# Three pairs of k-tiles made with seven products, in place of two, in the v and z_a products of an encoder layer

## The chip, the cores and the metric

The kernel runs on one core of one Trainium2 chip. The metric is the device time in microseconds (us) of one execution. A core has five engines with a queue of instructions each, worked off in order: TensorE (PE, matrix products), VectorE (DVE), ScalarE (ACT), GpSimd (POOL) and SyncE (SP, which here only issues DMAs). They wait for each other through semaphores. SBUF holds the tiles in 128 partitions, PSUM has eight banks in which matrix products add up, and 16 DMA engines move data between DRAM and SBUF, or within DRAM.

## The reference

One layer of a bidirectional encoder: 256 tokens, 2048 channels. Cut to what matters here:

```
hn   = rmsnorm(x, norm_w)
proj = hn @ w_in                         # (256, 2048) x (2048, 18432)
q, v, f_fwd, f_bwd, z_a, b_gate, c_gate, h_b, z_b = split(proj)    # 2048 columns each
o_a  = hgrn2_bidirectional(silu(q), v, f_fwd, f_bwd, lb)           # 16 heads of 128, chunks of 64
o_a  = head_rmsnorm(o_a) * silu(z_a)
y_b  = b_gate * conv3(c_gate * h_b);  o_b = rmsnorm(y_b) * silu(z_b)
h    = x + concat(o_a, o_b) @ w_out
h    = h + (p @ w_ple) * sigmoid(h @ w_ple_gate)
out  = rmsnorm(h, final_norm_w)
```

All is float32.

## The kernel before, in words

**Products.** A float32 operand is split into a high part, rounded to PE's fast float32r format, and the rest. A product is then three matmuls: high by high, high by low, low by high. `Stream.split` (L101, L102) makes the parts of the weights: ACT casts `raw` into the high half of an `spl` tile, DVE subtracts it from `raw` for the low half. `Stream.get` works four parts of 1024 columns ahead of PE; there are five `spl` buffers and three `raw` buffers of 1 MB. `Stream.load` issues the weight loads on SP (L80, or L76 for sums), in the order of use; a load waits until its `raw` buffer has been split.

**Order of the work.** The activations are held split in `xs` (16 k-tiles of 128). For i = 0, 2, 4, 6, `two_pairs(i)` makes two pairs of heads, i and i + 1. First come the forward and backward forget gates and q of both (`gemm_in`, L401 and L403; six products with 16 k-tiles each), then v and z_a of both pairs of heads at once. For i = 0 this is `gemm_two`; for i = 2, 4, 6 it is `gemm_vz`, a "v/z_a stage" below: 256 tokens (two halves m) by 512 columns of v and 512 of z_a (n). Between the products stand the chunkwise recurrence (`mix_forgets`, `mix_pair`, `outputs`) and the gate. Then follow the convolution branch, the output projection, the gate and the last norm.

**Pairs of k-tiles.** `gemm_vz` goes through eight pairs of k-tiles, q = 0 to 7, in that order. A plain pair takes 2 x 2 x 2 = 8 products (24 matmuls). A pair named in `VZ_SUMS` is treated as a 2 x 2 by 2 x 2 block product and made with seven (21 matmuls) in `half` (L523 to L525 are the matmuls in `three`): three go into the four main PSUM banks `avz` directly, and four into extra banks (`ex`, `ey` and the two `scps`), where all such pairs of a stage add up. After the last such pair, the extra banks are combined into `vt` and `zt` (one ACT copy; DVE L446 to L449). After the last pair, the main banks are added to them (L453) and scaled on ACT (L456); the first two additions free the two banks that the next `gemm_in` begins with. In the first and last pair of a stage, all products of v come before those of z_a. The main banks of z_a were used by q before, so the first product of z_a waits for q's evacuation (L464). Between the two stand the scores (L711) and the cross products `cx` (L755), which are put in at tick 4.

**Sums.** The seven products need sums of the activations and sums of the weights. Those of the activations are made once, in `xsums` (`act_sums`, L508 and L511; `act_split`, L518 and L519), into the tile `xsum`, through a scratch tile `xd`. Those of the weights are made in DRAM, in a tile `vz`: `prepare` copies the pair's four blocks (four DMAs of 256 KB on SP, L306), and `add_up` makes the sums with accumulating DMAs on POOL in three steps (step 0: two DMAs, L314; steps 1 and 2: one each, L318). Each step waits on POOL's queue for the landing of the one before. `Stream.add_sums` then lists the loads of such a pair: three blocks of `w_in` (0.75 MB) and the four blocks of sums (1 MB), 3.5 parts of 1024 columns where a plain pair has two.

**Due times.** `tick()` counts k-tiles (or groups of three matmuls); `at(dt, fn)` runs fn that many ticks later, in the order of the program. The sums for stage i + 2 are scheduled by `two_pairs(i)`: `prepare` of the z-th pair at tick 50 + 10z, its steps at ticks 166, 196 and 220 (+ z) for i > 0, and at 98 + 6 step + z for i = 0; the 158 ticks of a `two_pairs` put the former into the next one. `xsums(z)` is scheduled by `two_pairs(2)` at 10 + 12z. The planner below the program still moves instructions ahead of their place where an engine is free by its own estimate; the DMAs of `prepare` and `add_up` keep the program's order.

On POOL stand, besides L314 and L318: the multiplication by the norms (`by_norms`, L468), `kc`, `qc` and `kx` of `mix_pair` (L692, L698) and the gate (L593, L614). ACT makes the sigmoids and logarithms behind L468 (L590, L599), and DVE L603 and q's evacuation (L464) behind those.

Of the kernel before, what the change touches and what calls it, by code (L numbers as in the profile page):

```python
# [115 lines left out]
def tile_hymba_encoder(  # L116
# [32 lines left out]
    ws = Stream(tc, rawp, splp, 3)  # L149


    VZ_ORDER, VZ_SUMS = range(8), (2, 5)
    dramp = ctx.enter_context(tc.tile_pool(name="dramp", bufs=1, space=bass.MemoryType.DRAM))
    vz_prepared = {}
    blocks = {}
# [1087 lines left out]
```

## Time and profile before

| what | value |
|---|---|
| median of 3 runs | 1115.87 us (1114.24 to 1116.77) |
| profiled execution, first to last instruction (its span) | 1115.1 us, 0.77 us under the median |
| mean granted TensorE clock of the profiled execution | 0.997 |
| v/z_a stages (i = 2, 4, 6) in the profiled execution, from | about 194, 313 and 432 us |
| DMA over the span | 277.76 MB, mean 249 GB/s |

No separate time of the profiled execution is given beside its span, so the span stands for it. A row of a group gives line, engine, operation, tiles (out<-in), shapes and count; then busy us and the mean ns of one; then the idle time before it and what ended it. A row of the timeline gives start, duration, and in brackets the engine's idle time before it and its releaser. A row of the chain of waits gives start, duration and what ran, each step released by the one above it. "L102" is a line of the kernel. A matmul's duration is its whole passage through PE; the next one starts before it ends.

### The profile page before, as it was taken

The page shows a single profiled execution, that of the slowest core. Times are in us where ns is not written, and L with a number is a line of the kernel's source. Part 1 is how long each engine was busy: PE and PEld are TensorE (multiplying, and loading weights), DVE is VectorE, ACT ScalarE, POOL GpSimd, SP SyncE. Part 2 cuts the span into 40 slices and gives each one's busy share as a digit, 9 for nine tenths or more (in the row PEclk, how much of TensorE's full clock was granted, in tenths as well). Part 3 has the DMA queues.
Part 4 walks back from the last instruction along what each step waited for, and adds up shares of the span by engine and source line. Part 5 has one row for each costly group of instructions (what it writes and reads, how often), then busy time and mean ns, then how long its engine had stood idle before and what let it go on. Part 6 is the DMA issues. An engine that isn't in the chain of part 4 may idle for free.

```text
span 1115.1 us, 16970 instructions
## 1 busy us (share of the span) xinstructions
PE 1105.0 (99%) x6464; PEld 951.2 (85%) x6464; DVE 826.7 (74%) x1088; ACT 671.6 (60%) x939; POOL 291.5 (26%) x239
## 2 busy tenths in 40 slices
PE   9999999999999999999999999999999999999997
PEld 8888888888888888888888888888888888888886
DVE  7899467786887778797658748855758878877673
ACT  6787567666875697565535534534446565565562
POOL 1045325105530525043333223423331000000101
PEclk9999999999999999999999999999999999999998
DMA  9775985668778966858999998999979987887532
GB/s 348 273 249 192 223 266 179 217 227 213 234 207 306 303 172 182 279 180 206 296 312 252 263 335 218 294 311 266 298 201 296 332 287 284 297 305 254 196 132 76
DMA packets 79121, 277.76 MB, mean 249 GB/s; under 512 B 7872, under 2 KB 22080, under 8 KB 60736
## 3 DMA queue, kind: packets, MB, share of 16 engines
q1 hardware_dynamic: 64800, 253.26, 65.3%
q0 software_dynamic: 13952, 23.07, 13.6%
q8 instruction: 51, 0.84, 0.3%
q10 hardware_dynamic: 288, 0.34, 0.1%
q14 instruction: 30, 0.25, 0.1%
HBM read 274.55 MB, written 48.23 MB: 289 GB/s over the span
## 4 chain that ended last, share of the span: by engine, by line
PE 94%; ACT 2%; DMA 2%; POOL 1%; DVE 1%; issue 0%; DVEq 0%; ACTq 0%; POOLq 0%
PE a L403 34%; PE a L401 18%; PE avz L523 3%; PE avz L524 3%; PE avz L525 3%; PE pg L1004 3%; PE pg L1003 3%; PE pg L1005 3%; PE pa L523 2%; PE pa L524 2%; PE pa L525 2%; DMA raw<-in_w_in_dram 2%; PE a L424 1%; PE a L422 1%; PE a L423 1%; PE pb_sc L524 1%
## 5 line engine op out<-in xcount | busy, mean ns | idle before, releaser
L102 DVE TENSOR_TENSOR spl<-raw,spl 128x1024 fp32r<-128x1024 f32 (+2 forms) x413 | 505.7, 1238 | 190.1 <-ACT spl L101 187.5
L403 PE MATMUL a<-xs,spl 128*128 128x512 f32 x1792 | 624.6, 395 | 0.0
L101 ACT CAST spl<-raw 128x1024 fp32r<-128x1024 f32 (+2 forms) x413 | 409.0, 1001 | 250.6 <-PE a L401 88.1
L401 PE MATMUL a<-xs,spl 128*128 128x256 f32 x1792 | 496.8, 280 | 0.0
L403 PEld LDWEIGHTS a<-xs,spl 128*128 128x128 f32 x1792 | 334.6, 187 | 75.4
L401 PEld LDWEIGHTS a<-xs,spl 128*128 128x128 f32 x1792 | 337.5, 189 | 1.8
L1120 POOL TENSOR_TENSOR hh<-hh,fw 128x512 f32<-128x512 f32 (+1 forms) x9 | 11.0, 1228 | 250.7 <-ACT gt L1119 248.0
L523 PE MATMUL avz<-spl,xs 128*128 128x512 f32 x156 | 61.0, 391 | 0.6 <-DVE qt L464 0.6
L525 PE MATMUL avz<-spl,xs 128*128 128x512 f32 x156 | 60.7, 389 | 0.0
L524 PE MATMUL avz<-spl,xs 128*128 128x512 f32 x156 | 60.7, 389 | 0.0
L463 ACT COPY r<-a 128x256 f32<-128x256 f32 x112 | 40.4, 367 | 33.4 <-PE a L401 33.3
L692 POOL TENSOR_TENSOR qc<-pf,ge 128x256 f32<-128x256 f32 x16 | 23.2, 1453 | 106.5 <-ACT ge L679 95.6
L1003 PE MATMUL pg<-spl,ht 128*128 128x512 f32 (+1 forms) x120 | 45.2, 377 | 0.0
L1004 PE MATMUL pg<-spl,ht 128*128 128x512 f32 (+1 forms) x120 | 45.1, 376 | 0.0
L1005 PE MATMUL pg<-spl,ht 128*128 128x512 f32 (+1 forms) x120 | 45.0, 375 | 0.0
L468 POOL TENSOR_TENSOR xf<-xf,rbc 128x1024 f32<-128x1024 f32 x8 | 22.0, 2750 | 73.4 <-DVE rbc L379 49.4
L101 ACT CAST spl<-early 128x1024 fp32r<-128x1024 f32 (+1 forms) x29 | 28.7, 990 | 19.6 <-PE pb_y L525 7.5
L102 DVE TENSOR_TENSOR spl<-early,spl 128x1024 fp32r<-128x1024 f32 (+1 forms) x29 | 32.9, 1147 | 9.4 <-ACT spl L101 8.7
L920 POOL TENSOR_TENSOR cg<-cg,hb 128x512 f32<-128x512 f32 x8 | 14.6, 1826 | 80.6 <-DVE hb L464 80.6
L523 PEld LDWEIGHTS avz<-spl,xs 128*128 128x128 f32 x156 | 29.3, 188 | 6.9 <-DVE qt L464 0.8
L523 PE MATMUL pa<-spl,mixa 128*128 128x512 f32 x88 | 34.5, 392 | 0.0
L525 PEld LDWEIGHTS avz<-spl,xs 128*128 128x128 f32 x156 | 29.3, 188 | 6.1
(322 smaller groups left out, 1637.8 us busy)
## 6 DMA issues: line engine op xcount, KB each, us to landing
raw<-in_w_in_dram SPq DMA_DIRECT2D x106, 1024.0 KB, 7.4
raw<-in_w_in_dram SPq DMA_DIRECT2D x88, 256.0 KB, 4.1
raw<-in_w_out_dram SPq DMA_DIRECT2D x36, 512.0 KB, 5.2
sums<-in_w_out_dram SPq DMA_DIRECT2D x32, 512.0 KB, 11.4
raw<-in_w_in_dram SPq DMA_DIRECT2D x26, 512.0 KB, 7.0
raw<-sums SPq DMA_DIRECT2D x13, 1024.0 KB, 6.0
raw<-in_w_gate_dram SPq DMA_DIRECT2D x9, 1024.0 KB, 5.5
sums<-in_w_out_dram POOLq DMA_DIRECT2D x16, 512.0 KB, 10.0
```

What stands on the lines that cost most here:

```text
L101: self.nc.scalar.copy(out=v[:, :, 0], in_=r)
L102: self.nc.vector.tensor_tensor(out=v[:, :, 1], in0=r, in1=v[:, :, 0], op=ALU.subtract)
L401: pe.matmul(a[:, :T], lhsT=lhsT, rhs=xs[:, kt, 0, :], start=False, stop=(kt == NKT - 1))
L403: pe.matmul(a, lhsT=lhsT, rhs=xs[:, kt, :, :].rearrange("p s n -> p (s n)"), start=(kt == 0), stop=False)
L463: act.copy(out=r, in_=acc[m][:, 1, :])
L523: pe.matmul(acc, lhsT=ah, rhs=w[:, 0], start=start, stop=False)
L524: pe.matmul(acc, lhsT=ah, rhs=w[:, 1], start=False, stop=False)
L525: pe.matmul(acc, lhsT=al, rhs=w[:, 0], start=False, stop=stop)
L692: pool.tensor_tensor(out=c64(dst[:, d]), in0=c64(src[:, d, :, half * P : (half + 1) * P]), in1=g.unsqueeze(3).broadcast_to([P, 2, 2, CH]), ...
L1003: pe.matmul(acc[m], lhsT=lh, rhs=wh, start=(kt == 0), stop=False)
L1004: pe.matmul(acc[m], lhsT=lh, rhs=wl, start=False, stop=False)
L1005: pe.matmul(acc[m], lhsT=ll, rhs=wh, start=False, stop=(kt == nk - 1))
```

## The change

The pairs 2, 4 and 6 are made with seven products in place of 2 and 5. All else follows from the length and the values of `VZ_SUMS`: a third sum of weights for each of the three stages, a third group of activation sums (`xsum` grows from 8 to 12 KB in a partition), a third set of due times.

```diff
-    VZ_ORDER, VZ_SUMS = range(8), (2, 5)
+    VZ_ORDER, VZ_SUMS = range(8), (2, 4, 6)
```

## The prediction

> **What bounds the kernel now.** I read the page first, then PE's waits, then windows by stage, then the chain of waits around the stages that change. The page and PE's waits:
>
> ```profile
> PE 1105.0 (99%) x6464; PEld 951.2 (85%) x6464; DVE 826.7 (74%) x1088; ACT 671.6 (60%) x939; POOL 291.5 (26%) x239
> q1 hardware_dynamic: 64800, 253.26, 65.3%
> q0 software_dynamic: 13952, 23.07, 13.6%
> PE wps L242 <- DVE wz L237: 1.1, 1, 1.1
> PE avz L523 <- DVE qt L464: 0.6, 1, 0.6
> ```
>
> TensorE is busy for 99% of the span. After the start it waits for another engine only once that the trace names: 0.6 us, at the second product of one v/z_a stage. So whatever PE no longer has to do is gained, and whatever makes PE wait is lost, one for one. The windows below are, in order, the three v/z_a stages (i = 2, 4, 6), with the two heads of q and f in front of the second (columns: us, then busy time and count of PE, PEld, DVE, ACT, POOL, then clock, share of the DMA engines, GB/s).
>
> ```profile
> 194.00:238.50 44.50, 44.50 (x276) 36.93 (x275) 33.12 (x36) 28.12 (x34) 4.54 (x4) 1.00 0.69 231
> 238.50:318.00 79.50, 79.44 (x615) 69.71 (x613) 61.89 (x90) 60.25 (x94) 35.99 (x26) 1.00 0.74 209
> 318.00:362.50 44.50, 43.92 (x199) 36.56 (x200) 34.73 (x39) 27.75 (x32) 4.54 (x4) 1.00 0.81 277
> 437.00:478.50 41.50, 41.50 (x188) 34.49 (x187) 31.72 (x34) 25.32 (x29) 6.01 (x7) 1.00 0.75 247
> ```
>
> The granted clock is 1.00, DVE is busy about three quarters of each v/z_a stage (33.12 of 44.50 us), and the DMA engines 0.69 to 0.81.
>
> **What the change removes.** Of a pair of k-tiles, eight products of three matmuls become seven: 24 matmuls become 21. The PE timeline of stage i = 4 has both kinds side by side: a pair with seven products runs from its first `ex` matmul at 326.88 to 331.63, the plain pair behind it to 337.07.
>
> ```profile
> 326.88 0.39 PE L523 MATMUL ex<-spl,xs 128*128 128x512 f32 x1
> 331.63 0.39 PE L523 MATMUL avz<-spl,xs 128*128 128x512 f32 x1
> 337.07 0.39 PE L523 MATMUL avz<-spl,xs 128*128 128x512 f32 x1
> ```
>
> The first is 4.75 us for 21, the second 5.44 us for 24, both 0.2265 us from start to start; the 0.39 us in the rows is one matmul's whole passage, and pricing by it would give 3.5 us, too much. One more such pair in each of three stages: 9 x 0.2265 = 2.04 us less PE work. That is all the change can give, apart from a wait that vanishes.
>
> **What it adds to DVE and ACT.** The third pair's activations are summed once (xsum), from rows of the two that exist:
>
> ```profile
> L511 DVE TENSOR_TENSOR xd<-xd x8: 280/288/1275, 45.8 to 60.8; 128x128 f32<-128x128 f32 x8
> L508 DVE TENSOR_TENSOR xd<-xs x2: 680/686/692, 45.1 to 46.9; 128x512 f32<-128x512 f32 x2
> L518 ACT CAST xsum<-xd x2: 614/614/615, 50.5 to 65.5; 128x512 fp32r<-128x512 f32 x2
> L519 DVE TENSOR_TENSOR xsum<-xd,xsum x2: 678/678/679, 58.4 to 74.8; 128x512 fp32r<-128x512 f32 x2
> 75.00:116.00 41.00, 41.00 (x346) 34.54 (x345) 37.69 (x47) 30.37 (x47) 23.86 (x20) 1.00 0.65 217
> ```
>
> DVE: 0.69 + 4 x 0.288 + 0.68 = 2.5 us, ACT 0.6 us. They share one scratch tile with the second pair's, whose last row starts at 74.8, so they fall in the stretch behind it, where DVE is busy 37.69 of 41 us. Its 3.3 us of idle time can hold them; if they land ahead of weight splits, PE could be late by at most 2.5 us. I take 0.2.
>
> A pair made with seven products splits 3.5 units of 1024 columns in place of 2:
>
> ```profile
> L102 DVE TENSOR_TENSOR spl<-raw,spl 128x1024 fp32r<-128x1024 f32 x369 | 477.0, 1303 | 186.3 <-ACT spl L101 183.7
> L102 DVE TENSOR_TENSOR spl<-raw,spl 128x512 fp32r<-128x512 f32 x40 | 28.1, 726 | 3.9 <-ACT spl L101 3.8
> ```
>
> On DVE 3 x 1.30 + 0.73 = 4.6 us against 2.6 us, under 4.75 us of PE time. In a stage DVE goes from about 33 to 35 of 44 us. No cost, with DVE's remaining 9 us as the cover.
>
> The pair's results are put together by one ACT copy and four DVE operations right after the last pair with seven products. That pair was 5, with two plain pairs (10.9 us) behind it; now it is 6, with one (5.44 us).
>
> ```profile
> 347.51 0.68 DVE L446 TENSOR_TENSOR xd<-vt,scps 128x512 f32<-128x512 f32 x1
> 350.44 0.68 DVE L449 TENSOR_TENSOR zt<-zt,scps 128x512 f32<-128x512 f32 x1
> 355.14 1.28 DVE L453 TENSOR_TENSOR vt<-avz,vt 128x512 f32<-128x512 f32 x2
> ```
>
> From the first to the end of the fourth is 3.6 us, one weight split among them. The two additions that free the first two PSUM banks (L453, 1.28 us) need these results. 3.6 + 1.3 = 4.9 us fits into 5.44 with half a microsecond over; one more split (1.2 us) in between costs 0.7 us in each stage. I take 0.2 in all; the end is 2.1.
>
> **What it adds to POOL and the DMA queues.** The third sum adds, for each stage, four copies from DRAM to DRAM on SP (1 MB), four accumulating DMAs of 256 KB on POOL in three steps (two, one, one), and 0.75 MB more to load. Where does that meet the path? The one PE wait is the place. The chain of waits that leads to it:
>
> ```profile
> 260.55 1.06 ACT spl L101
> 261.64 1.24 DVE spl L102
> 262.89 16.82 DMA raw<-in_w_in_dram
> 279.79 1.05 ACT spl L101
> ...
> 306.63 0.44 POOL kx L698
> 307.08 0.55 issue
> 307.63 1.67 POOL vz L318 x2
> 309.30 2.44 POOL xf L468
> ...
> 318.19 0.34 DVE qt L464
> 318.58 0.50 PE avz L523
> ```
>
> A weight load took 16.8 us, ACT got it late, and from there ACT, DVE and POOL pass the delay on for 38 us until q's evacuation frees PE's bank late. Two rows price that. ACT waited for the load at 279.79:
>
> ```profile
> 279.79 1.05 ACT L101 CAST spl<-raw 128x1024 fp32r<-128x1024 f32 x1 [0.82 <-DMA raw<-in_w_in_dram]
> 436.21 1.09 PE cx L755 x8
> 437.30 0.30 PE avz L523
> ```
>
> In stage i = 6, whose ACT has no such wait, PE goes from the cross products (436.21, eight) straight on at 437.30. So 0.82 us of ACT's wait became 0.64 us of PE's: the chain has 0.18 us of slack, and what comes on top is paid in full. Two things come on top.
>
> First, POOL issues three L318 where it issued two, between kx and the multiplication by the norms (xf L468). Two took 1.67 us on the chain, 0.83 each; in POOL's own rows the first starts at 307.63 and L468 at 308.72, 0.55 each. I take 0.55, in i = 4 in full, in i = 6 less the 0.18 of slack: 0.4. The stage i = 2 has its steps long before and pays nothing. Behind the waiting L318 of step 1, POOL's next work has cover:
>
> ```profile
> 274.71 0.85 POOL L318 DMA_DIRECT2D vz<-vz  x1 [4.22 <-DMA vz<-in_w_in_dram]
> 283.13 1.29 POOL L468 TENSOR_TENSOR qt<-qt,rbc 128x512 f32<-128x512 f32 x1 [7.58 <-DVE gx L677]
> ```
>
> A third wait there may last to 283 before anyone needs POOL.
>
> Second, the load itself. It was in flight while the step 0 DMAs of this stage and the copies for the next one were:
>
> ```profile
> 256.53 4.24 POOL L314 DMA_DIRECT2D vz<-in_w_in_dram  x4
> 262.00:270.00 8.00, 8.00 (x122) 7.04 (x121) 4.12 (x6) 4.45 (x6) 4.93 (x4) 1.00 1.13 246
> 270.00:278.00 8.00, 8.00 (x54) 7.22 (x52) 6.08 (x10) 7.06 (x13) 1.34 (x2) 1.00 0.96 250
> ```
>
> DMA share 1.13 and 0.96: full. Four L314 become six, 0.52 MB more. POOL's queue costs 13.6% of 1115.1 us for 23.07 MB, 6.6 us of all engines per MB: 3.45 us. The load is later by nothing if it gets through ahead of them, by 3.45 us if all of it goes first; both queues share the engines, so I take two thirds, nearer the upper end because the engines are full: 2.2 us. All of that reaches PE. The third copy for the next stage is issued 10 ticks behind the second, after the loads that matter here; in i = 6 no copies for a next stage stand beside step 0, and ACT had no wait for a load, so I charge nothing there.
>
> The Trainium skill's page "DMA: Bandwidth & Descriptors", section "Queues, rings and completion order", says that each DMA engine takes turns between the queues that have work, a packet at a time. By that rule POOL's packets do not simply go ahead of the load's, which supports a value between the two ends and against none. The same page's fit for a POOL DMA (section "Anatomy of one DMA"), 2.0 us plus bytes over 436 GB/s, would make 0.52 MB cost the engines about 1.2 us of movement (an estimate from that page) and two thirds of that, 0.8 us in place of 2.2, would bring the sum to 0.1 us above before, between my forecast and the second rival below; the trace's 6.6 us per MB speaks against that price for DMAs that accumulate.
>
> **The sum**, against the profiled execution's span of 1115.1 us: -2.04 (PE) + 0.55 + 0.4 (POOL) + 2.2 (load) + 0.2 (xsum) + 0.2 (end of stage) = +1.5 us, 1116.6. The median of the runs lies 0.8 us over the span, so 1117.4 us. A change under 0.2% (2.2 us) can hardly be told from none here, so this is no measurable change, on the slow side.
>
> **Rivals.**
> 1. *Slower: the late load is paid in full.* If step 0's extra 3.45 us all go ahead of the load, and ACT then also waits for the load behind it, the wait at i = 4's second product grows to about 4.6 us: -2.04 + 0.55 + 0.4 + 3.45 + 0.4 = +2.8 us, 1118.7 us; with one split in the way at each end of a stage another 2.1 us, 1120.8. It decides from a delay of 2.9 us on. For it: a share of 1.13, and a chain with no slack. Against: the load's queue was served all along. 0.40.
> 2. *The DMAs fit.* The load comes no later: -2.04 + 0.55 + 0.4 + 0 = -1.1 us, 1114.8 us. For it: POOL's two added DMAs queue behind four others. It shares the chance of "no change" with my forecast, 0.48 together, of which 0.14 is this one.
> 3. *Faster: the wait goes.* The stage in front is 0.68 us shorter, the engines' orders shift, and the load no longer falls into the full stretch: -2.04 - 0.64 = -2.7 us, 1113.2 us. Nothing in the rows moves these DMAs apart, 0.12.
>
> That the change doesn't do what it says would show as 24 matmuls for pair 4 or 6; the code leaves no room for it.
>
> **How the numbers follow.** Forecast 1117.4 us, no change 0.48, slower 0.40, faster 0.12. The likeliest case's own range is 1113.7 to 1118.1. The range, 1113.2 to 1122.0, reaches from the third rival to a little over the first with every end of a stage late.
>
> **What would show it.** Right: nine matmuls fewer; PE's wait at the second product of stage i = 4 between 2.5 and 4 us, with ACT's wait for a load near 280 grown from 0.82 to about 3; about 0.4 us of wait at i = 6; three L318 ahead of xf L468; no wait at the first f matmul after a v/z_a stage. Wrong: no growth of ACT's wait for the load, waits where a stage ends, or a wait near 100 us, where the splits are behind.

## The result, and the profile after

The change makes the kernel slower: 1123.26 us (median of 6 runs, 1120.16 to 1125.21) against 1115.99 us (6 runs of the kernel before, 1114.24 to 1116.77). The ratio is 1.0064, interval 1.0052 to 1.0075; the medians lie 7.3 us apart, and the new one lies outside the predicted range. The profiled execution of the changed kernel took 1121.36 us with a span of 1119.6 us, one of the quicker ones, so its span shows 4.5 us of the loss.

The page after (engines; then the two DMA queues: packets, MB, share of 16 engines) and PE's waits (us in total, times, longest):

```profile
PE 1102.5 (98%) x6455; PEld 948.5 (85%) x6455; DVE 832.8 (74%) x1100; ACT 676.5 (60%) x946; POOL 300.5 (27%) x251
q1 hardware_dynamic: 69264, 258.76, 65.7%
q0 software_dynamic: 16448, 26.22, 15.5%
```

```profile
PE avz L523 <- DVE qt L464: 2.9, 2, 1.9
PE avz L524 <- DVE spl L102: 1.8, 1, 1.8
...
PE cx L755 <- POOL kx L698: 1.1, 1, 1.1
PE a L401 <- DVE spl L102: 0.7, 1, 0.7
PE ogt L634 <- DVE ogz L624: 0.6, 1, 0.6
```

PE has nine matmuls fewer (6455 for 6464) and 2.5 us less busy time. But where it waited once after the start, for 0.6 us, it now waits six times, for 7.1 us in all (2.9 + 1.8 + 1.1 + 0.7 + 0.6). The work removed was as predicted; new waits are over three times as large. The PE timeline places the end points of the ledger below:

```profile
112.40 1.16 PE L755 MATMUL cx<-qc,kx 128*128 128x128 f32 x8 [1.06 <-POOL kx L698]
241.89 0.40 PE L403 MATMUL a<-xs,spl 128*128 128x512 f32 x1
323.78 0.50 PE L523 MATMUL avz<-spl,xs 128*128 128x512 f32 x1 [1.91 <-DVE qt L464]
342.28 0.39 PE L523 MATMUL ex<-spl,xs 128*128 128x512 f32 x1
352.48 0.39 PE L523 MATMUL ex<-spl,xs 128*128 128x512 f32 x1
442.84 0.50 PE L523 MATMUL avz<-spl,xs 128*128 128x512 f32 x1 [1.01 <-DVE qt L464]
```

```profile
241.60 0.40 PE L403 MATMUL a<-xs,spl 128*128 128x512 f32 x1
437.11 0.50 PE L523 MATMUL avz<-spl,xs 128*128 128x512 f32 x1
```

The first fence is after, the second before. From the first `ex` matmul of pair 4 to that of pair 6 lie 10.20 us: 45 matmuls (21 of a pair with seven products, 24 of the plain pair 5) at 0.2267 us, the predicted price. Early in the first product of the forget gates for i = 4, PE is 0.29 us later than before (241.89 against 241.60). At the second product of stage i = 4 it is 5.20 us later (323.78 against 318.58). So between these two points, which hold no matmul that the change touches, 4.9 us were lost. At the second product of i = 6 it is 5.73 us later, after 0.68 us gained in stage i = 4: 1.21 us more lost by then.

The chain of waits to the second product of stage i = 4 has the same steps as before, from another load:

```profile
272.28 20.42 DMA raw<-in_w_in_dram
292.78 1.05 ACT spl L101
...
311.05 1.05 POOL kx L698
312.10 2.43 POOL vz L318 x3
314.53 2.42 POOL xf L468
...
323.40 0.34 DVE qt L464
323.78 0.50 PE avz L523
```

A load issued at 272.28 takes 20.4 us, ACT gets it at 292.78, and the delay goes through ACT, DVE, POOL (three L318 between kx and xf) and q's evacuation to PE. ACT's own row, from its timeline, says how long it stood:

```profile
292.78 1.05 ACT L101 CAST spl<-raw 128x1024 fp32r<-128x1024 f32 x1 [4.93 <-DMA raw<-in_w_in_dram]
```

That is 4.93 us where before shows 0.82, at the load in front of this one: 4.1 us more. With one more L318 in the chain (2.43 us for three against 1.67 for two, 0.8 us) this makes 4.9 us, what PE lost between the two points.

What delays the load is read from the two queues while it was in flight, 272.4 to 286.3 before and 272.3 to 292.7 after (packets, MB, share of the 16 engines; before is the upper fence):

```profile
q1 hardware_dynamic: 1575, 3.93, 84.4%
q0 software_dynamic: 298, 0.53, 21.6%
```

```profile
q1 hardware_dynamic: 1911, 4.33, 62.5%
q0 software_dynamic: 1229, 1.54, 45.9%
```

In both the two queues fill the engines. What went through SP's queue (q1) in that time is nearly the same: 84.4% of 13.9 us is 11.7 us of all engines before, 62.5% of 20.4 us is 12.8 after. But after, POOL's queue (q0) has twice the share, and SP's takes longer for much the same work. The Trainium skill's page "DMA: Bandwidth & Descriptors", section "Queues, rings and completion order", has the engines take turns between the queues, a packet at a time. The trace agrees in so far as both queues move at once; it shows no fixed shares (62.5 to 45.9 here, 34.7 to 76.7 in e7 below).

### The profile page after: what moved, and what is told of

Its sections match the earlier page's. It is cut to its first block, busy times and chain, and to the rows that moved or that the text cites. A ratio compares the mean times of both kernels' runs of the same rounds, so it can differ in the third digit from the quotient of the medians.

```text
span 1119.6 us, 17020 instructions
## 1 busy us (share of the span) xinstructions
PE 1102.5 (98%) x6455; PEld 948.5 (85%) x6455; DVE 832.8 (74%) x1100; ACT 676.5 (60%) x946; POOL 300.5 (27%) x251
## 3 DMA queue, kind: packets, MB, share of 16 engines
q1 hardware_dynamic: 69264, 258.76, 65.7%
q0 software_dynamic: 16448, 26.22, 15.5%
## 4 chain that ended last, share of the span: by engine, by line
PE 78%; DVE 8%; POOL 5%; ACT 3%; DMA 2%; issue 2%; SPq 0%; DVEq 0%; ACTq 0%; POOLq 0%
PE a L403 28%; PE a L401 15%; DVE spl L102 3%; PE pg L1004 3%; PE pg L1005 3%; PE pg L1003 3%; PE avz L523 2%; PE avz L525 2%; PE avz L524 2%; DMA raw<-in_w_in_dram 2%; PE pa L523 2%; PE pa L524 2%; PE pa L525 2%; POOL kc L692 1%; POOL xf L468 1%
## 5 line engine op out<-in xcount | busy, mean ns | idle before, releaser
L101 ACT CAST spl<-raw 128x1024 fp32r<-128x1024 f32 (+2 forms) x419 | 414.0, 999 | 251.2 <-PE a L401 92.5
L401 PE MATMUL a<-xs,spl 128*128 128x256 f32 x1792 | 496.5, 280 | 0.7 <-DVE spl L102 0.7
L401 PEld LDWEIGHTS a<-xs,spl 128*128 128x128 f32 x1792 | 337.6, 189 | 3.2 <-DVE spl L102 1.3
L523 PE MATMUL avz<-spl,xs 128*128 128x512 f32 x138 | 54.1, 392 | 2.9 <-DVE qt L464 2.9
L524 PE MATMUL avz<-spl,xs 128*128 128x512 f32 x138 | 53.8, 390 | 1.8 <-DVE spl L102 1.8
L525 PE MATMUL avz<-spl,xs 128*128 128x512 f32 x138 | 53.8, 390 | 0.0
L468 POOL TENSOR_TENSOR xf<-xf,rbc 128x1024 f32<-128x1024 f32 x8 | 22.6, 2828 | 70.9 <-DVE rbc L379 48.8
L523 PE MATMUL pa<-spl,mixa 128*128 128x512 f32 x88 | 34.5, 392 | 0.0
L524 PE MATMUL pa<-spl,mixa 128*128 128x512 f32 x88 | 34.3, 390 | 0.0
L525 PE MATMUL pa<-spl,mixa 128*128 128x512 f32 x88 | 34.3, 390 | 0.0
```

The costliest lines, as they stand in the source:

```text
L101: self.nc.scalar.copy(out=v[:, :, 0], in_=r)
L401: pe.matmul(a[:, :T], lhsT=lhsT, rhs=xs[:, kt, 0, :], start=False, stop=(kt == NKT - 1))
L468: pool.tensor_tensor(out=t, in0=t, in1=r.unsqueeze(1).broadcast_to([P, n, T]), op=ALU.mult)
L523: pe.matmul(acc, lhsT=ah, rhs=w[:, 0], start=start, stop=False)
L524: pe.matmul(acc, lhsT=ah, rhs=w[:, 1], start=False, stop=False)
L525: pe.matmul(acc, lhsT=al, rhs=w[:, 0], start=False, stop=stop)
```

## The experiments

Ratios are against the kernel before on the same chip, with 95% intervals; line numbers in some kernels stand one to four higher than in the listing. The theory at this point: the DMAs of the third weight sum delay the load, and ACT, DVE and POOL hand the delay to PE. The rivals: more work on DVE and ACT (splits, `xsum`); and the ends of the stages, where one plain pair is left in place of two.

### Without the third weight sum: e1_sums_shared

```diff
-                    sums = dramp.tile([P, 4, 512], F32, name=f"vz{i}_{q}")
-                    vz_prepared[i].append((srcs, sums))
+                    if q == 6:
+                        sums = vz_prepared[i][1][1]
+                    else:
+                        sums = dramp.tile([P, 4, 512], F32, name=f"vz{i}_{q}")
+                        vz_prepared[i].append((srcs, sums))
```

> Pairs 2, 4 and 6 with seven products, but the third pair's weight sums are not made: pair 6 loads the sums of pair 4 (that part of the output is wrong). All matmuls, splits, activation sums and loads are those of the changed kernel; the third sum's four copies and four accumulating DMAs per stage are gone. Theory (the third sum's DMAs delay a weight load of the heads before stage i = 4, and POOL's third L318 adds 0.5 us): most of the loss goes; left are -2.0 us of PE work, +1.4 us near 106 us and about +0.5 us at the ends of stages: within 1 us of the kernel before, 1115 to 1117 us; ACT's wait for a load near 280 us back under 1 us. Rival (the extra DVE and ACT work of the third pair makes the loss): 1121 to 1124 us as the changed kernel.

1116.06 us, ratio 0.9986 (0.9971 to 1.0002). By the ratios this is 8.7 us less than the change. ACT waits for no load between 265 and 305, the load of that place took 12.8 us, and of PE's waits after the start and up to the stages' end these are left:

```profile
PE cx L758 <- POOL kx L701: 1.1, 1, 1.1
PE avz L526 <- DVE qt L467: 0.2, 1, 0.2
```

All splits, loads and matmuls of the third pair are there; only the making of the sums is not. So these DMAs make the loss at i = 4. The 1.1 us at `cx` stay as they were in the change and must have another cause.

### The third sum made and not used: e2_dmas_alone

In the kernel before, pair 6 stays plain, but its weight sum is made:

```diff
+                if q == 6:
+                    vz_prepared[i].append((srcs, dramp.tile([P, 4, 512], F32, name=f"vz{i}_{q}")))
```

> The kernel before (pairs 2 and 5), and beside it a third sum of weights (of pair 6) is made in DRAM for each stage at the changed kernel's due times, but nothing reads it. Theory: the loss of the DMAs alone shows without any gain: +5 to +7 us against the kernel before, 1121 to 1123 us, with PE's wait at the second product of stage i = 4 at 4 us or more in place of 0.6. Rival (the work on DVE and ACT makes the loss): +0 to +1.5 us, 1116 to 1117.5 us.

1123.33 us, ratio 1.0043 (1.0027 to 1.0059). Nothing is added to PE, and nothing to DVE and ACT, and the waits around stage i = 4 are the change's (ACT's timeline, then PE's waits):

```profile
292.10 1.05 ACT L101 CAST spl<-raw 128x1024 fp32r<-128x1024 f32 x1 [5.00 <-DMA raw<-in_w_in_dram]
```

```profile
PE avz L525 <- DVE qt L466: 2.6, 2, 1.9
PE avz L526 <- DVE spl L102: 1.8, 1, 1.8
```

The rival of DVE's and ACT's work falls for the wait at i = 4. The DMAs alone cost 4.8 us (3.0 to 6.6), a little less than the 5 to 7 expected.

### Without the third group of activation sums: e3_no_third_xsum

The changed kernel, with pair 6 reading pair 4's activation sums (the two lines that point it there and shrink `xsum` are left out here):

```diff
-            for z in range(len(VZ_SUMS)):
+            for z in range(2):
```

> The changed kernel without the third group of activation sums: pair 6 uses those of pair 4 (that part of the output is wrong). 2.5 us of DVE work and 0.6 us of ACT work between 75 and 110 us are gone. Theory (these sums cost 1.4 us near 106 us, since the splits there have no slack left): 1.4 us faster than the changed kernel, 1120 to 1122.5 us, with PE's waits before 125 us as in the kernel before. Rival (they are hidden, and the shift near 106 us has another cause): 1123 us as the changed kernel.

1122.62 us, ratio 1.0043 (1.0026 to 1.0060). Its interval overlaps that of the change (1.0052 to 1.0075), so the time alone doesn't settle the third `xsum`. The trace does: the wait of `cx` for kx is gone from PE's waits, while those of i = 4 stay (`avz` 1.7 for a split). So the third group of sums makes the wait at 112 us.

### The last pair moved, without a third: e4_pairs_2_6

```diff
-    VZ_ORDER, VZ_SUMS = range(8), (2, 5)
+    VZ_ORDER, VZ_SUMS = range(8), (2, 6)
```

> Two pairs with seven products as before, but 2 and 6 in place of 2 and 5. Only the place of the second pair moves: its combination on DVE has one plain pair behind it, not two. Theory (the ends of the stages cost 0.2 to 0.5 us in all): +0 to +1 us against the kernel before, 1115.5 to 1117 us. Rival (the late combination holds up each stage's end by a split or more): +2 us or more, 1118 us, with PE's waits at the first f product behind each stage.

1115.77 us, ratio 0.9988 (0.9974 to 1.0002). One plain pair is left behind the last sum, as in the change, and PE waits at no end of a stage. Even before's 0.6 us is missing here: that small wait comes and goes between programs with equal DMAs. The ends of the stages as such are no cause.

### Which of the DMAs: e5_copies_alone and e6_copies_step0

Both are e2 with the third sum begun and not finished: `prepare` alone, or `prepare` and step 0 (two of its four accumulating DMAs). The lines below are e5's; e6 has `step >= 1`.

```diff
+                    if z == 2 and step >= 0:
+                        continue
```

> The kernel before, and of a third sum only its four copies from DRAM to DRAM per stage (1 MB, on SP), at the changed kernel's due times; no accumulating DMAs, nothing reads it. Theory (POOL's step 0 DMAs ahead of the load issued near 272 us are what delays it; the third copies are issued behind the loads that matter): within 1 us of the kernel before. Rival (the copies load the engines as much as the accumulation and make half of the loss): +2 us or more.

> As e5, and step 0 of the third sum as well (two accumulating DMAs of 256 KB per stage on POOL); no steps 1 and 2. Theory: step 0 carries most of the loss: +3 to +5 us against the kernel before, with ACT's wait for a load near 285 us at 3 us or more; missing against all the DMAs alone are POOL's third L318 ahead of the multiplication by the norms (0.55 us in i = 4, 0.4 in i = 6) and step 1's share of the engines. Rival (the loss sits in steps 1 and 2, that is in POOL's waiting): within 1 us of the kernel before.

e5: 1115.59 us, ratio 0.9998 (0.9988 to 1.0008). e6: 1120.94 us, ratio 1.0035 (1.0016 to 1.0054). The same load in e5, then in e6, with ACT's wait for it in e6:

```profile
raw<-in_w_in_dram SPq DMA_DIRECT2D x1, 1024.0 KB, 15.0
```

```profile
raw<-in_w_in_dram SPq DMA_DIRECT2D x1, 1024.0 KB, 19.2
```

```profile
291.23 1.05 ACT L101 CAST spl<-raw 128x1024 fp32r<-128x1024 f32 x1 [4.17 <-DMA raw<-in_w_in_dram]
```

The copies, 1 MB for each stage, cost nothing: they are issued behind the loads that matter. Step 0, 0.5 MB on POOL's queue, brings the delay (14.0 us before, 15.0 with copies, 19.2 with step 0) and most of the loss. PE's wait at i = 6 is absent in e6, so it belongs to steps 1 and 2.

### The copies moved out of the way: e7_copies_later and e8_before_copies_later

The load stands on SP's queue behind eight copies of the first two sums for stage i + 2, issued between 258 and 268, just when step 0 for stage i runs. e7 is the changed kernel, e8 the kernel before, with all copies 30 ticks later:

```diff
-                at(50 + 10 * z, lambda what=what: prepare(what))
+                at((80 if i else 50) + 10 * z, lambda what=what: prepare(what))
```

> The changed kernel with the copies for the next stage due at ticks 80, 90 and 100 in place of 50, 60 and 70 (for i > 0). All the work is kept; copies and step 0 no longer stand beside each other in front of stage i = 4. Theory (copies and step 0 together fill the engines and delay the loads by 20 us): the wait for the load goes, what is left of the loss is POOL's third L318 (1 us) and 1.4 us near 106 us, against 2.0 us gained: 1115 to 1118 us. Rival (POOL's accumulation alone delays the loads): 1121 us or more.

> The kernel before (pairs 2 and 5) with the same later due times of the copies. Theory: PE's 0.6 us of wait at stage i = 4 goes and nothing else changes: -0.3 to -1 us against the kernel before. Rival (the copies then delay the loads of the v/z_a stages instead): slower by 1 us or more, with PE waits inside a v/z_a stage.

e7: 1117.95 us, ratio 1.0017 (1.0007 to 1.0027). e8: 1116.51 us, ratio 1.0003 (0.9994 to 1.0012). The load in e7, and what is left of PE's waits at the second products:

```profile
raw<-in_w_in_dram SPq DMA_DIRECT2D x1, 1024.0 KB, 7.9
```

```profile
PE avz L523 <- DVE qt L464: 1.7, 2, 1.0
```

All six accumulating DMAs of step 0 still run, and the load takes 7.9 us in place of 20.4. In e8, with four of them, it takes 6.8. So neither step 0 nor the copies do it alone. While e7's load was in flight (274.8 to 282.7), SP's queue had even less of the engines than in the changed kernel:

```profile
q0 software_dynamic: 702, 0.99, 76.7%
q1 hardware_dynamic: 146, 1.06, 34.7%
```

But 34.7% of 7.9 us is 2.7 us of all engines, for little more than the load itself (1.06 MB), where 11.7 and 12.8 us went through SP's queue with the copies in front. Without them 5.2 us of the loss are gone (1.0064 less 1.0017). The kernel before, with four accumulating DMAs in step 0 and not six, gains nothing that can be measured, though PE's 0.6 us of wait is gone from e8's trace: the -0.3 to -1 us expected don't show. The waits at 112 us and at i = 6 stay.

### The rest of the loss: e9_and_xsum_later, e10_and_step2_early, e11_two_pairs_both_moves, e12_changed_again

e9 is e7 with the third group of activation sums kept in its place in the program, tick 34 of i = 2. e10 is e9 with step 2 of stages 4 and 6 issued ahead of POOL's kc in place of behind kx. e11 has pairs 2 and 5 with the copies later and step 2 early. e12 is the change again. The lines below are those of e9 and, behind the dots, of e10; the line that skips step 2 in its old place is left out.

```diff
-                act_sums(xs[:, k : k + 2], a, t)
+                act_sums(xs[:, k : k + 2], a, t, tc.keep_in_program_order if z == 2 else lambda instr: instr)
...
                     if before:
                         before()
+                    for what in vz_prepared[i] if i > 2 else ():
+                        add_up(what, 2)
```

> The changed kernel with the copies due later (as e7), and the third group of activation sums kept at its place in the program (tick 34 of i = 2, about 145 us, where DVE is half idle). Theory (they cost 1.4 us near 106 us): 1.4 us faster than with the copies alone moved: 0 to -1 us against the kernel before, with no shift of PE near 106 us. Rival (the shift there comes from elsewhere, or the sums cost as much at 145 us): as e7, +1.9 us.

> As e9, and step 2 of the sums for i = 4 and 6 is issued on POOL ahead of kc, in 3.6 us in which POOL waits for DVE, in place of between kx and the multiplication by the norms. Theory (each L318 there costs PE 0.55 to 0.83 us at the second product of stages i = 4 and 6): -2 to -3 us against the kernel before, 0.998, with no PE wait for DVE's qt; this would be the version that beats both kernels. Rival (those waits are made by DVE's or ACT's work): as e9.

> The kernel before (pairs 2 and 5) with the two moves that apply to it: copies later and step 2 ahead of kc. Theory (two L318 and the late load were all that PE waited for): -0.5 to -1 us against the kernel before, 0.9993; the third pair (e10) is then worth 2 us with everything else alike. Rival (the moves speed up two pairs as much as three): -2 us.

> The changed kernel itself, on the same chip as the three above. Theory: 1.0064 as measured, between 1.004 and 1.008, and between 1118 and 1126 us from one execution to the next, since the late load's delay differs. Rival (its loss is a matter of the chip): outside that.

| kernel | median us | ratio | interval |
|---|---|---|---|
| e9, + third xsum later | 1117.86 | 1.0004 | 0.9990 to 1.0018 |
| e10, + step 2 early | 1116.54 | 0.9994 | 0.9982 to 1.0005 |
| e11, two pairs, both moves | 1116.33 | 0.9991 | 0.9979 to 1.0003 |
| e12, the change | 1124.19 | 1.0061 | 1.0041 to 1.0081 |

e12 repeats the loss. Its profiled execution has a span 2.9 us longer than that of after, and shows a part that after's lacks: behind PE's wait at the second product of i = 4 the granted clock is 0.50 for some 3.4 us, and eight matmuls start 0.43 us apart in place of 0.23, 1.6 us more (columns as in the prediction's windows; e12, then after):

```profile
327.00:330.00 3.00, 3.00 (x9) 2.32 (x8) 3.00 (x5) 2.55 (x5) 1.73 (x3) 0.50 0.71 247
327.00:330.00 3.00, 3.00 (x15) 2.49 (x14) 3.00 (x4) 2.06 (x4) 2.96 (x3) 1.00 0.25 93
```

Four of the fourteen profiled executions have such a stretch around this stage's second product (e3, e6, e10, e12), and how often it comes in the other runs isn't recorded. So what PE loses at this place is at times more than its wait; what decides it isn't shown.

In e9 the wait of `cx` is gone, as in e3. In e10 the one of i = 6 is gone as well, but the one at i = 4 grows from 0.7 us in e9 to 1.7 (PE's waits, then the loads issued from 299 to 303):

```profile
PE avz L523 <- DVE qt L464: 1.7, 1, 1.7
```

```profile
raw<-in_w_in_dram SPq DMA_DIRECT2D x4, 256.0 KB, 12.1
```

Step 2 (issued from 294 on) now meets the later copies (issued from 295 to 297), and the next group of loads pays (ACT waits 2.93 us for one of them): 12.1 us for 256 KB, where the changed kernel's loads of that size, issued at 305 to 307, take 3.9. The moves together bring the third pair back to the time of before and no further; the -2 to -3 us expected of e10 fail. With the same moves, three pairs (e10) and two (e11) take the same time within their intervals: in the profiled execution of e10, 1.7 us go into this one wait and 1.6 into the matmuls at half the clock behind it, more than the third pair's 2.0 us. No kernel here is faster than before by more than its interval.

## Why the prediction was wrong, step by step

The kind of mechanism was predicted, a late load handed on through ACT, DVE and POOL, and so were the nine matmuls. What failed above all is the term of the load: it was worked out for another load, and by a rule for the delay that doesn't hold. Every other term of cost was too small as well.

- **PE, -2.04: right.** 45 matmuls in 10.20 us, and nine fewer of them.
- **The load, 2.2: the step that failed.** The prediction followed the load issued at 262.89, whose lateness the chain of before showed, and gave it two thirds of 3.45 us. In after that load takes 16.0 us (before 16.8) and ACT no longer waits for it. It is the next one, issued at 272, that goes from 14.0 to 20.4 us, and ACT's wait for a load from 0.82 to 4.93 us: 4.1 us in place of 2.2, and above the bound of 3.45. The bound was wrong too: it took step 0's engine time alone as the delay. The load grew by 6.4 us, because steps 0 and 1 of three sums follow each other on POOL's queue and leave SP's 62.5% of the engines in place of 84.4%, while the load stands behind eight copies on its own (e5, e6, e7). The prediction had this load as "the load behind it" in its first rival, without a price of its own. The fit of the Trainium skill's page "DMA: Bandwidth & Descriptors", section "Anatomy of one DMA", which would have made the term 0.8 us (an estimate from that page), is further off still. Step 1's waits on POOL's queue (timeline of after) show how long that queue stayed busy:

```profile
259.11 6.32 POOL L314 DMA_DIRECT2D vz<-in_w_in_dram  x6
280.10 0.84 POOL L318 DMA_DIRECT2D vz<-vz  x1 [6.57 <-DMA vz<-in_w_in_dram]
284.76 0.81 POOL L318 DMA_DIRECT2D vz<-vz  x1 [3.82 <-DMA vz<-in_w_in_dram]
```

  The third wait ends at 284.76, with 283 named as the latest time at which nobody needs POOL; the multiplication behind it (L468) started at 285.31, still ahead of the load that ACT waited for.
- **L318, 0.55 and 0.4: too small.** On the chain three take 2.43 us in i = 4 and two took 1.67: 0.76, not 0.55. The chain's own row (0.83 each) was the nearer one, as it counts what POOL's successor waits for. At i = 6 PE lost 1.21 us and not 0.4; one more L318 explains some 0.8 (three take 2.45 us on the chain there). The experiments tell the remaining 0.4 apart: by PE's timelines e2, with the third sum and none of the third pair's work, loses 0.9 us there, and e1, with the work and not the sum, 0.4. So it comes with the pair's own work; which instruction makes it was not followed.
- **xsum, 0.2: wrong.** PE loses 1.4 us at the third group of activation sums. The prediction had named "a wait near 100 us, where the splits are behind" as a sign against it. The cover it took, 3.3 us of idle time of DVE between 75 and 116, is an average over two stretches. Cut at 100.2, where DVE reaches the product that kc waits for, the same trace of before says (columns as above, DVE third):

```profile
72.00:100.20 28.20, 28.20 (x207) 23.52 (x206) 28.00 (x43) 22.95 (x31) 10.55 (x9) 1.00 0.63 208
100.20:116.00 15.80, 15.80 (x157) 13.63 (x156) 12.69 (x13) 10.20 (x20) 13.30 (x11) 1.00 0.76 263
```

  28.00 of 28.20 us are busy ahead of that point; all the idle time lies behind it. After, DVE's rows for the third group stand in the full part, and POOL's kc starts later by them (timeline after; the last row is before's kc):

```profile
75.57 0.49 DVE L511 TENSOR_TENSOR xd<-xd 128x128 f32<-128x128 f32 x2
77.11 0.61 DVE L511 TENSOR_TENSOR xd<-xd 128x128 f32<-128x128 f32 x2
91.74 0.68 DVE L519 TENSOR_TENSOR xsum<-xd,xsum 128x512 fp32r<-128x512 f32 x1
102.33 3.35 POOL L692 TENSOR_TENSOR kc<-dd,ge 128x256 f32<-128x256 f32 x1 [6.21 <-DVE pf L684]
```

```profile
100.89 3.35 POOL L692 TENSOR_TENSOR kc<-dd,ge 128x256 f32<-128x256 f32 x1 [6.22 <-DVE pf L684]
```

  The three rows make 1.78 us; kc is 1.44 us later, though PE ran 0.55 us earlier than before at that place. PE loses 1.44 us by the product behind the cross products, 1.06 us of it as the wait for kx. The place was right ("the stretch behind it"), its price was not: what matters there is DVE's own path, not whether weight splits come late.
- **Ends of the stages, 0.2: a little small.** At i = 6 one split (478.23) does get between the four operations, as the prediction had it, and the first additions (L453) start at 481.15, late by a part of a microsecond:

```profile
478.23 1.22 DVE L102 TENSOR_TENSOR spl<-raw,spl 128x1024 fp32r<-128x1024 f32 x1
```

```profile
481.51 0.39 PE L525 MATMUL avz<-spl,xs 128*128 128x512 f32 x1
481.98 0.47 PE L403 MATMUL a<-xs,spl 128*128 128x512 f32 x1
```

  The next product begins 0.47 us behind the last matmul, where 0.23 is the pace; with the second bank 0.5 us are lost. At i = 2 it is 0.2 us, at i = 4 nothing. With two pairs (e4) nothing of this shows.

Added up, the rows of after give -2.0 + 1.4 + 4.9 + 1.2 + some 0.7 for the ends of two stages = +6.2 us, where the prediction had +1.5. The two spans differ by 4.5 us. Matmul by matmul, most of the rest lies where the change touches no product: PE of after is 0.6 us earlier from the start stretch on, and before loses 1.3 us against it between 740 and 850 us, without a wait that the trace names. The start stretch shifts by -0.8 to +1.6 us between executions of the kernels here. The medians differ by 7.3 us: the profiled execution of after is 1.9 us under its median, and the stretch at half the clock that e12 shows would account for most of that, but no trace of the slower executions of after was kept.

Of the rivals the first had the right sign and place, and at 1118.7 to 1120.8 us too low a price; the others fall: the DMAs don't fit, and no wait goes away.

Of the signs that were listed as right, three L318 and nine matmuls are there. PE's wait at the second product of i = 4 is 1.9 us, under the 2.5 to 4; with 1.8 us for a split in the first product it is 3.7, and 1.3 us more are lost between 298 and 303 (the waits of L401 and L634), from the same late load. ACT's wait for the load near 280 did not grow: it went, and came at the next load. Of the signs listed as wrong, the wait near 100 us is there, at 112, and two ends of stages are late by parts of a microsecond.

## What to carry to other kernels

Where two queues share full engines, the time of a transfer is the engine time of what stands in front of it on its own queue and its own, divided by the share that is left (12.8 us at 62.5% made 20.4 us here); the engine time added to the other queue is no bound for the delay. Look at everything queued ahead of it, and at the load behind the one on the chain too. Idle time of an engine is a cover only up to the instruction that someone waits for; cut the window there before counting on it. Work taken from the engine that is busy 99% of the time is gained only if nothing is paid for it through queues whose slack was already spent.

## What the runs showed of the hardware that was not expected

The 1 MB load at the same place in the program took between 6.8 and 20.4 us depending on 0.5 MB of accumulating DMAs on POOL's queue and on copies ahead of it on SP's. With eight copies ahead it took 14.0 us beside four accumulating DMAs of step 0 and 20.4 beside six; with the copies out of the way 6.8 and 7.9. So two sets of DMAs that were bearable one at a time cost PE 4.9 us together. The engine time of accumulating DMAs was as dear as predicted: 3.15 MB more on q0 took 15.5% of 1119.6 us in place of 13.6% of 1115.1, 6.9 us per MB, where q1 paid 2.8 (65.7% of 1119.6 us for 258.76 MB). And in four of the fourteen traces, close to a wait of PE at stage i = 4, the clock granted to PE is 0.50 for some 3.4 us, which cost 1.6 us in e12.
